# Half of the softmax scalings of an attention kernel, moved from ScalarE to GpSimd

## The chip, the cores and the metric

One core of one Trainium2 chip runs the whole program. The metric is the device time of one execution in microseconds (us); of several executions the median is given. Where a profile is read, it is one execution that the hardware profiler recorded. The engines are TensorE (PE in the rows, its weight loads PEld), VectorE (DVE), ScalarE (ACT), GpSimd (POOL), and SyncE (SP), which here issues DMAs.

## What is computed

Two layers of a gated block over 528 tokens (16 meta tokens and 512 of the input) of width 1024. Each layer normalizes, projects, and adds the output of two branches. Branch A is attention of 8 heads of 64 over one shared key and value head; a small indexer first selects for each query the 128 best visible keys. The part that the change touches is the softmax:

```python
logits = jnp.einsum('bqhd,bqkd->bqhk', qb, kg).astype(jnp.float32) * attn_scale
logits = jnp.where(valid[:, :, None, :], logits, NEG_INF)
p = jax.nn.softmax(logits, axis=-1).astype(vg.dtype)
return jnp.einsum('bqhk,bqkd->bqhd', p, vg)
```

Branch B is a pooling over several windows. Both are gated by `sigmoid(merge)` and go through an output projection. Everything is float32; the kernel splits operands of its large products into a rounded part and a residue.

## The kernel before

The dense products of a layer run one after the other on TensorE, in groups that accumulate in PSUM. Attention is not a stage of its own: it is a generator (`attention`), whose steps are pulled in between the groups of two other stages, the product of branch B (`zb`) and the gates (`mix_gates`). After each group or half group, `half_done` adds to a credit and pulls steps by it. The program order of TensorE and of VectorE is the order in which the code is traced (`tc.manual_schedule`); for ScalarE and GpSimd a scheduler puts the instructions in order by their priorities and dependences, but each instruction stays on its engine.

Attention treats four blocks of 128 queries, and in each block four pairs of heads: 16 units in a layer. Here they are numbered 0 to 15 in the first layer and 16 to 31 in the second. In block i the visible keys are n = 144, 272, 400, 528 (`NK`). For a unit (block i, pair j) the steps are:

- `logits`: TensorE, queries times keys of both heads, into PSUM banks "a".
- `soft`: VectorE adds the mask of the selection (`SC`) and takes the minimum, into the tile L of each head (128 x n in SBUF). ScalarE takes the exponential in place and sums it (line 907).
- `scale`: VectorE takes the inverse of the two sums (`rs`, line 916). ScalarE multiplies the columns from 16 on of each head's L by it, in place (line 918). The first 16 columns, the meta tokens, are multiplied into the tile `pm` (line 919), on GpSimd for the first three pairs of a block and on VectorE for the fourth.
- `turn`: TensorE transposes L in blocks of 128 columns, alternating between the two heads of the pair, into banks "a"; ScalarE copies them out (`pt`, line 934). After the fourth pair `meta_turn` does the same with `pm`.
- `values`: TensorE multiplies by the values.

One step of the generator holds the `logits` of the next unit and the `scale` of this one, the second the next unit's `soft`, the third this unit's `turn`.

In the same stretches the weights of the gates are prepared (`mixed_prep`): ScalarE rounds blocks of them (line 254), VectorE forms residues and sums of blocks, and GpSimd issues DMAs that add one block to another in SBUF (`sum_by_dma`, line 159), which are kept in program order on its queue. VectorE's instructions go through a helper that counts their cost, so all of them have line 60 in the profile, and so have TensorE's.

Of the kernel before, what the change touches and what calls it, by code (L numbers as in the profile page):

```python
# [10 lines left out]
AF = mybir.ActivationFunctionType  # L11
OP = mybir.AluOpType
# [75 lines left out]
def tile_block(ctx: ExitStack, tc: tile.TileContext, x, meta, w_in, pool_w, w_a, w_b, w_out, rows, hgain, c_tab, out):  # L88
    nc = tc.nc
    act, gp = nc.scalar, nc.gpsimd  # L90
    pe, dve = Metered(nc.tensor, pe_cost), Metered(nc.vector, dve_cost)
# [404 lines left out]
    def small(n, name):  # L496
        return tmp.tile([128, n], F32, tag=f"sm{n}", name=name, bufs=6)
# [375 lines left out]
    def attention(ensure):  # L873
        st, pvs, pms, turned = {}, {}, {}, []
# [36 lines left out]
        def scale(u):  # L911
            i, j = divmod(u, 4)
            n = NK[i]
            L, sm = st[u]
            rs = small(2, "rs")
            dve.reciprocal(rs, sm)
            for hh in range(2):
                act.activation(L[hh][:, 16:n], L[hh][:, 16:n], AF.Copy, scale=rs[:, hh:hh + 1])
                (gp if j < 3 else dve).tensor_scalar(pms[i][:, 2 * j + hh, :], L[hh][:, 0:16], rs[:, hh:hh + 1], None, op0=OP.mult)  # L919
            st[u] = L  # L920

        def turn(u):
# [43 lines left out]
        for u in range(-1, 17):  # L966
            if u + 1 < 16:
                logits(u + 1)
            if 0 <= u < 16:
                scale(u)  # L970
            yield
            if u + 1 < 16:
                soft(u + 1)
            if u >= 1:
                turned.append(u - 1)
                if u % 4 == 0 or (u > 8 and u % 2 == 0):
                    while turned:
                        values(turned.pop(0))
                if u % 4 == 0:
                    meta_values(u // 4 - 1)  # L980
            yield
            if u >= 1 and u % 4 == 0:
                gated(u // 4 - 1)
            if 0 <= u < 16:
                turn(u)
                if u % 4 == 3:
                    meta_turn(u // 4)
            yield
# [381 lines left out]
    for l in range(2):  # L1370
# [107 lines left out]
        for c in range(2):  # L1478
            w = chunk()
            for mi in range(2):  # L1480
                j = 2 * c + mi
# [42 lines left out]
        for c in (1, 0):  # L1524
            w = chunk()
            for mi in (1, 0):
                j = 2 * c + mi
# [24 lines left out]
        for c in range(2):  # L1552
            w = chunk()
            for mi in range(2):
                j = 2 * c + mi
# [26 lines left out]
        for c in range(2):  # L1582
# [3 lines left out]
            for mi in range(4):  # L1586
                j = 4 * c + mi
# [28 lines left out]
        for c in range(2):  # L1616
            w = chunk()
            for mi in range(4):
                j = 4 * c + mi
# [76 lines left out]
        else:  # L1696
            work, operands = sums_of_y(ta)
            for c in range(2):
                w = chunk()
                for t in range(1, 5):  # L1700
# [6 lines left out]
                    for e, (jj, k) in enumerate(steps):  # L1707
                        h, ww = ((hhi, w[0]), (hhi, w[1]), (hlo, w[0]))[jj]
# [60 lines left out]
```

## Time and profile before

| | us |
|---|---|
| median of 3 runs | 739.24 |
| lowest and highest | 738.99 and 739.27 |
| the profiled execution | 738.92 |
| its span, first to last instruction | 737.1 |

The granted clock of TensorE is 0.999 of full speed over the span. Busy times in the span: TensorE 727.4 us, VectorE 565.0, ScalarE 476.4, GpSimd 240.8. In the rows, a timeline's line gives the start, the duration, the engine, the line of the kernel, the operation, what it writes and reads, the sizes, how many were merged into the row, and in brackets the idle time of the engine before it with what ended that. The ends of matmuls are modelled, so matmuls overlap in the rows.

### The profile page before, as it was taken

To read this page: it belongs to the slowest core of one execution; us is meant where nothing else is said; L and a number is where in the kernel's file an instruction comes from. 1 tells how busy PE (TensorE), PEld (TensorE's weight loads), DVE (VectorE), ACT (ScalarE), POOL (GpSimd) and SP (SyncE) were. 2 spreads that over 40 slices of the span, in tenths; PEclk is the share of its full clock that TensorE was granted. 3 is DMA by queue.
4 is the path that set the end of the run, shared out by engine and by line. 5 is a ranking of instruction groups with operands and counts; after the bars stand their busy time and mean duration, and the time that the engine had idled before them with its cause. 6 is when DMAs were issued, how large, how long until landed. Compare 5 with 4: busy or idle time off the path is not lost.

```text
span 737.1 us, 15803 instructions
## 1 busy us (share of the span) xinstructions
PE 727.4 (99%) x5886; PEld 695.4 (94%) x5886; DVE 565.0 (77%) x1431; ACT 476.4 (65%) x1058; POOL 240.8 (33%) x318
## 2 busy tenths in 40 slices
PE   8999999999999999999999999999999999999998
PEld 7899999999999999999998989988989999999997
DVE  5976997889888765794549768987997777758885
ACT  5878645649878795543246687455587887864641
POOL 3850065244113120063346411751521111303500
PEclk9999999999999999999999999999999999999999
DMA  8777666777254345643604869768943544446552
GB/s 271 233 164 191 148 144 172 172 182 179 51 122 99 85 104 127 198 145 109 158 1 116 174 171 227 188 146 201 203 106 88 129 107 97 96 121 235 147 147 72
DMA packets 111036, 107.37 MB, mean 146 GB/s; under 512 B 21696, under 2 KB 93152, under 8 KB 110960
## 3 DMA queue, kind: packets, MB, share of 16 engines
q1 hardware_dynamic: 99648, 74.76, 34.2%
q0 software_dynamic: 10944, 31.46, 23.7%
q8 instruction: 46, 0.75, 0.4%
q14 instruction: 30, 0.25, 0.1%
q10 hardware_dynamic: 368, 0.15, 0.1%
HBM read 66.41 MB, written 8.49 MB: 102 GB/s over the span
## 4 chain that ended last, share of the span: by engine, by line
PE 82%; ACT 5%; DVE 4%; DMA 3%; issue 3%; POOL 2%; SPq 0%; DVEq 0%; POOLq 0%; ACTq 0%
PE d L60 66%; PE a L60 13%; PE v L60 3%; DMA raw<-s 1%; DMA raw<-in_w_in_dram 1%; ACT lt L907 1%; DVE w L60 1%; ACT w L254 1%; ACT pt L934 0%; DVE nf L60 0%; POOL t L721 0%; DVE lt L60 0%; DVE t L60 0%; POOL rk L524 0%; ACT hhi L553 0%
## 5 line engine op out<-in xcount | busy, mean ns | idle before, releaser
L60 PE MATMUL d<-hhi,w 128*128 128x256 f32 (+3 forms) x1408 | 287.5, 296 | 0.7 <-DVE rs L60 0.4
L60 PEld LDWEIGHTS d<-hhi,w 128*128 128x128 f32 x1408 | 226.0, 188 | 6.8 <-DVE c L60 0.9
L60 PE MATMUL d<-hlo,w 128*128 128x256 f32 (+3 forms) x704 | 193.6, 294 | 0.0
L60 PEld LDWEIGHTS d<-hlo,w 128*128 128x128 f32 x704 | 132.8, 189 | 2.5 <-issue 0.2
L60 DVE TENSOR_TENSOR w<-raw,w 128x512 fp32r<-128x512 f32 (+1 forms) x128 | 106.6, 853 | 5.2 <-ACT w L254 4.9
L60 PE MATMUL d<-hsum,w 128*128 128x264 f32 (+1 forms) x576 | 76.6, 286 | 0.3 <-ACT p L1143 0.3
L60 PEld LDWEIGHTS d<-hsum,w 128*128 128x128 f32 x576 | 71.7, 188 | 0.9 <-ACT p L1143 0.5
L60 PE MATMUL d<-w,hhi 128*128 128x256 f32 x496 | 72.4, 286 | 0.0
L221 POOL DMA_DIRECT2D w<-raw x42 | 37.4, 903 | 100.3 <-ACT w L220 84.1
L60 PEld LDWEIGHTS d<-w,hhi 128*128 128x128 f32 x496 | 64.1, 188 | 4.0 <-issue 1.8
L254 ACT CAST w<-raw 128x512 fp32r<-128x512 f32 x96 | 57.2, 626 | 4.1 <-DMA raw<-s 4.1
L159 POOL DMA_DIRECT2D raw<-s x17 | 15.0, 883 | 125.2 <-DVE s L60 42.1
L60 DVE MATCH_REPLACE8 sc<-m,sc 128x400 f32<-128x400 f32 (+2 forms) x100 | 54.3, 549 | 0.0
L60 DVE MAX8 m<-sc 128x8 f32<-128x400 f32 (+2 forms) x100 | 52.7, 557 | 0.8
L907 ACT ACTIVATE lt<-lt,mn,NR 128x144 f32<-128x144 f32 (+3 forms) x64 | 42.4, 666 | 15.9 <-DVE mn L60 15.9
L919 POOL TENSOR_SCALAR pm<-lt,rs 128x16 f32<-128x16 f32 x48 | 22.7, 489 | 81.8 <-DVE rs L60 74.3
L220 ACT ACTIVATE w<-raw 128x1024 fp32r<-128x1024 f32 x42 | 44.1, 1063 | 7.5 <-PE d L60 7.5
L60 PE MATMUL d<-mhi,w 128*128 128x272 f32 (+2 forms) x192 | 47.6, 328 | 0.0
L225 ACT CAST w<-raw 128x1024 fp32r<-128x1024 f32 x42 | 43.7, 1050 | 0.0
L1627 POOL TENSOR_TENSOR hlo<-ta,hhi 128x256 fp32r<-128x256 f32 (+1 forms) x28 | 28.2, 1018 | 42.1 <-PE d L60 28.9
L60 PE MATMUL d<-w,hlo 128*128 128x256 f32 x248 | 38.5, 281 | 0.0
L60 PE MATMUL d<-ahi,w 128*128 128x256 f32 (+1 forms) x256 | 36.0, 282 | 0.0
(265 smaller groups left out, 1542.0 us busy)
## 6 DMA issues: line engine op xcount, KB each, us to landing
w<-raw POOLq DMA_DIRECT2D x42, 512.0 KB, 5.9
raw<-in_w_in_dram SPq DMA_DIRECT2D x40, 512.0 KB, 4.9
raw<-in_w_in_dram SPq DMA_DIRECT2D x72, 256.0 KB, 3.3
raw<-in_w_out_dram SPq DMA_DIRECT2D x16, 512.0 KB, 3.7
raw<-in_w_branch_b_dram SPq DMA_DIRECT2D x8, 512.0 KB, 4.8
raw<-raw POOLq DMA_DIRECT2D x16, 256.0 KB, 4.2
raw<-s POOLq DMA_DIRECT2D x16, 256.0 KB, 3.3
raw<-in_w_branch_a_dram SPq DMA_DIRECT2D x8, 512.0 KB, 3.8
```

The lines of the kernel that those rows point to most:

```text
L60: return fn(*a, **k)
L159: tc.keep_in_program_order(gp.dma_start(to, x, accum_op=OP.add))
L220: act.activation(t, raws[c][s], AF.Copy, scale=-1.0)
L221: gp.dma_start(t, raws[c][s], accum_op=OP.add)
L225: act.copy(t, raws[c][s])
L254: act.copy(t[:, 0], blk[src[n]])
L907: act.activation(L[hh][:, :n], L[hh][:, :n], AF.Exp, scale=NR[:, i, h:h + 1], bias=mn[:, hh:hh + 1], accum_out=sm[:, hh:hh + 1])
L919: (gp if j < 3 else dve).tensor_scalar(pms[i][:, 2 * j + hh, :], L[hh][:, 0:16], rs[:, hh:hh + 1], None, op0=OP.mult)
L1627: pool_end = gp.tensor_sub(hlo[:, j, a:a + n], d, f(hhi[:, j, a:a + n]))
```

## The change

In `scale`, the second head's multiplication of the columns from 16 on goes to GpSimd as a tensor_scalar with the same operands. The first head's stays on ScalarE. The two narrow multiplications into `pm` stay on their engines and are traced after both wide ones, where before each stood behind the wide one of its own head.

```diff
             for hh in range(2):
-                act.activation(L[hh][:, 16:n], L[hh][:, 16:n], AF.Copy, scale=rs[:, hh:hh + 1])
-                (gp if j < 3 else dve).tensor_scalar(pms[i][:, 2 * j + hh, :], L[hh][:, 0:16], rs[:, hh:hh + 1], None, op0=OP.mult)
+                if hh:
+                    gp.tensor_scalar(L[hh][:, 16:n], L[hh][:, 16:n], rs[:, hh:hh + 1], None, op0=OP.mult)
+                else:
+                    act.activation(L[hh][:, 16:n], L[hh][:, 16:n], AF.Copy, scale=rs[:, hh:hh + 1])
+            for hh in range(2):
+                h = 2 * j + hh
+                (gp if j < 3 else dve).tensor_scalar(pms[i][:, h, :], L[hh][:, 0:16], rs[:, hh:hh + 1], None, op0=OP.mult)
             st[u] = L
```

## Rows read from the trace of the kernel before

**Rows 1.** The page's busy times, share of the span, and instructions, by engine.

```profile
PE 727.4 (99%) x5886; PEld 695.4 (94%) x5886; DVE 565.0 (77%) x1431; ACT 476.4 (65%) x1058; POOL 240.8 (33%) x318
```

**Rows 2.** Table by stretches: busy us and instructions by engine, clock, DMA share, GB/s.

```profile
170.00:290.00 120.00, 119.71 (x1058) 117.22 (x1057) 93.39 (x273) 97.70 (x247) 25.82 (x41) 1.00 0.45 103
530.00:650.00 120.00, 118.76 (x965) 111.98 (x965) 93.00 (x271) 98.32 (x240) 27.32 (x43) 1.00 0.48 107
sum 240.00, PE 238.47 PEld 229.21 DVE 186.40 ACT 196.02 POOL 53.14; mean PE 119.24 PEld 114.60 DVE 93.20 ACT 98.01 POOL 26.57
```

**Rows 3.** Timeline of TensorE in the second layer's stretch.

```profile
582.50 0.35 PE L60 MATMUL d<-hhi,w 128*128 128x256 f32 x1 [0.36 <-DVE rs L60]
...
618.36 0.51 PE L60 MATMUL a<-KK,qq 128*128 128x256 f32 x2 [0.75 <-ACT ptm L952]
618.71 1.58 PE L60 MATMUL d<-hsum,w 128*128 128x256 f32 x12
```

**Rows 4.** The same two stretches, line 918 alone: the row of sums.

```profile
sum 240.00, ACT 32.91; mean ACT 16.46
```

**Rows 5.** Line 919: duration in ns, least, median and most.

```profile
L919 POOL TENSOR_SCALAR pm<-lt,rs x48: 318/328/1192, 173.8 to 634.6; 128x16 f32<-128x16 f32 x48
```

**Rows 6.** GpSimd's groups by form: count, busy us, mean ns, idle before.

```profile
L1539 POOL TENSOR_TENSOR us<-us 128x541 f32<-128x541 f32 x6 | 6.5, 1090 | 0.5
...
L1542 POOL TENSOR_TENSOR us<-us,consts 128x16 f32<-128x16 f32 x8 | 1.8, 223 | 0.5
```

**Rows 7.** Timeline around the scaling of unit 15, several engines.

```profile
272.23 0.90 POOL L159 DMA_DIRECT2D raw<-s  x1 [5.95 <-ACT pt L934]
272.35 0.16 DVE L60 RECIPROCAL rs<-sm 128x2 f32<-128x2 f32 x1
...
272.83 1.20 POOL L159 DMA_DIRECT2D raw<-raw  x1
...
273.76 0.69 DVE L60 TENSOR_TENSOR w<-raw,w 128x512 fp32r<-128x512 f32 x1
...
274.47 1.03 PE L60 MATMUL a<-consts,lt 128*128 128x128 f32 x8
```

**Rows 8.** Waits of ScalarE in the second stretch: us, times, longest.

```profile
ACT w L254 <- DMA raw<-s: 0.7, 2, 0.4
```

**Rows 9.** Timeline of VectorE and GpSimd at two places.

```profile
169.24 1.44 DVE L60 TENSOR_SCALAR NR<-RQ 128x8 f32<-128x8 f32 x1
169.57 1.07 POOL L721 TENSOR_TENSOR t<-t,t 128x256 f32<-128x256 f32 x1
...
264.60 1.27 DVE L60 TENSOR_TENSOR w<-raw,w 128x512 fp32r<-128x512 f32 x2
264.80 1.49 POOL L919 TENSOR_SCALAR pm<-lt,rs 128x16 f32<-128x16 f32 x2 [5.29 <-DVE rs L60]
```

**Rows 10.** Timeline around the scaling of unit 23.

```profile
582.27 0.16 DVE L60 TENSOR_SCALAR NR<-RQ 128x8 f32<-128x8 f32 x1
582.34 0.16 DVE L60 RECIPROCAL rs<-sm 128x2 f32<-128x2 f32 x1
582.42 1.21 POOL L159 DMA_DIRECT2D raw<-raw  x1
...
583.75 0.42 DVE L60 SCALAR_TENSOR_TENSOR zb<-th,zb 128x256 f32<-128x256 f32 x1
...
583.97 0.60 PE L60 MATMUL a<-consts,lt 128*128 128x128 f32 x4
```

**Rows 11.** Timeline around the scaling of unit 21.

```profile
568.78 0.15 DVE L60 RECIPROCAL rs<-sm 128x2 f32<-128x2 f32 x1
...
570.28 0.69 DVE L60 TENSOR_TENSOR w<-raw,w 128x512 fp32r<-128x512 f32 x1
...
570.97 0.60 PE L60 MATMUL a<-consts,lt 128*128 128x128 f32 x4
```

**Rows 12.** Timeline around the scaling of unit 31.

```profile
643.19 0.16 DVE L60 RECIPROCAL rs<-sm 128x2 f32<-128x2 f32 x1
...
646.38 1.03 PE L60 MATMUL a<-consts,lt 128*128 128x128 f32 x8
```

## Prediction

> **What bounds the kernel now.** The first view is the page's line of busy times: TensorE is busy for 727.4 of 737.1 us [rows 1]. The second is the table by stretches for the two places where the changed lines run, one for each layer, 120 us long each. TensorE is busy for 119.71 and 118.76 us in them, ScalarE for 97.70 and 98.32, VectorE for 93.39 and 93.00, GpSimd for 25.82 and 27.32 [rows 2]. So in the stage of the change TensorE sets the time, and what it lacks to fullness is 0.29 + 1.24 = 1.53 us. Work that leaves ScalarE can give back no more than TensorE's waits. The third view, TensorE's timeline, shows the largest of these: 0.75 us before the logits of unit 29 at 618.36, released by a ScalarE copy, and 0.36 us at 582.50, released by VectorE [rows 3]. The ends of matmuls are modelled: twelve in a row take 1.58 us, so one follows the other after about 0.12 us while one alone is drawn with 0.28 [rows 3]. A wait can therefore be up to 0.16 us longer than its gap; with some five waits in the two stretches, 1.53 + 5 x 0.16 = 2.3 us is the most that there is to win.
>
> **What the change removes.** 32 of the 64 scalings on ScalarE. All 64 take 32.91 us, so about 16.5 us leave ScalarE, 8.2 in each stretch of 120 [rows 4]. One takes 32.91 / 64 = 0.51 us on average, and what follows it in ScalarE's queue (casts of weights, copies of transposed probabilities, the next exponentials) can start that much earlier, until ScalarE next waits for another engine. In the waits of [rows 3] little hangs on that: one was released by VectorE, and the other by a copy that stands behind the two exponentials of its unit, which had to wait for other things than a scaling. I take a gain between 0 and 2.3 us and 0.8 in the sum, since most of TensorE's waits end with work that no scaling precedes directly.
>
> **What it adds.** 32 scalings of 128, 256, 384 and 512 columns on GpSimd, eight of each size. The trace has no such instruction there. The same kind with 16 columns takes 318 ns at best and 328 in the median [rows 5]; with two tensors GpSimd takes 223 ns for 16 columns and 1090 for 541 [rows 6], which is 867 / 525 = 1.65 ns a column. From above, with that slope on top of the 0.32 us, 512 columns take 0.32 + 496 x 1.65 = 1.14 us, 384 0.93, 256 0.72 and 128 0.50. From below, with half the slope, since one tensor is read and not two: 0.73, 0.63, 0.52 and 0.41. I take the middle. The sum is 8 x (0.41 + 0.52 + 0.63 + 0.73) = 18 to 26 us, or 9 to 13 in a stretch in which GpSimd idles for over 92 [rows 2]. Room is not the question.
>
> **What it moves.** The two scalings of a unit ran one behind the other on ScalarE; now they run side by side. The narrow multiplications of a unit (16 columns) are issued behind the wide one, which costs nothing: their reader is one transpose for four units. In the last unit of each four, GpSimd had no such work; now it waits for the inverse sums there too, and the weight sums that it issues as DMAs may queue behind that wait, or it behind them. Each issue holds GpSimd for 0.9 to 1.2 us [rows 7]. A sum that is issued up to 1.1 us later lands later by as much; ScalarE's casts, which wait for the landings, sat idle for them for 0.7 us in all in the second stretch [rows 8], so most of that is covered.
>
> **Where the new instruction is late.** Every unit's transposes on TensorE alternate between the two heads, so the second transpose, 0.11 us behind the first (eight in a row take 1.03 us, so 1.03 / 8 = 0.13 at most) [rows 7], waits for GpSimd. In unit 15 the inverse sums start at 272.35 and the transposes at 274.47, so GpSimd has until 274.58. There it issues DMAs from 272.23 to 273.13 and from 272.83 to 274.03, and VectorE multiplies and subtracts two SBUF tensors until 274.45 [rows 7]. What a subtraction with two SBUF inputs does to GpSimd is in [rows 9]: two of them, back to back from 264.60 to 265.87, stretch a pair of 16-column multiplications that started at 264.80 to 1.49 us, past their end. So GpSimd's wide scaling starts between 273.13 (it goes between the two DMAs and ahead of VectorE) and 274.45, and ends between 273.86 and 275.59: TensorE waits between 0 and 1.0 us. Unit 23 (256 columns): sums at 582.34, VectorE with such pairs until 584.17, transposes from 583.97, due 584.08 [rows 10]. GpSimd ends between 582.42 + 0.52 (if it goes ahead of the DMA issue there), in time, and 584.17 + 0.72 = 584.89: 0 to 0.8 us. Unit 21: sums at 568.78, VectorE's train to 570.97, transposes from 570.97, due 571.08 [rows 11]; late by 0 to 570.97 + 0.72 - 571.08 = 0.6 us. Units 6 and 25 repeat that pattern with 0 to 0.3 each. The other 27 units have more cover. The last, unit 31, stands for them: sums at 643.19, transposes at 646.38 [rows 12], so 3.3 us to the second one, where a DMA issue and a scaling of 1.14 fit. Together 0 to 3.0 us of new waits on TensorE; I take the middle, 1.5.
>
> **The other direction of the same collision.** GpSimd also holds VectorE. An 8-column tensor_scalar, 0.16 us alone [rows 10], took 1.44 us from 169.24 on and ended at 170.68, while GpSimd's addition of two tensors ran from 169.57 to 170.64 [rows 9]. In the last unit of each four VectorE has two such narrow ones right behind the inverse sums, and behind them stand the weight residues and the next unit's minima. 32 instructions of 0.4 to 1.1 us can hold VectorE for 0 to 26 us in total, but it idles for 240 - 186.4 = 53.6 us in the two stretches [rows 2], and TensorE's products are ready ahead of it nearly everywhere; I put it into the slower rival, at nothing in the sum. The Trainium skill has this as a rule (SBUF — State Buffer, section "SBUF: two separate sides"): VectorE and GpSimd have a pair of ports in common, it is an exclusive lock, and whichever starts first keeps it for its whole instruction. By that rule the stretched pair of [rows 9] is what one expects, and the trace agrees. The rule speaks against the change; the slower rival is what it would do here.
>
> **The sum.** On the profiled execution's own time of 738.92 us (span 737.1 and 1.8 around it): 738.92 + 1.5 - 0.8 = 739.6. The median of the runs lies 0.32 above that execution, so 739.9 us.
>
> **Rivals.** (1) Slower: GpSimd loses to VectorE's trains each time. Its place is the five units named above, its price all of 1.0 + 0.8 + 0.6 + 0.3 + 0.3 = 3.0 us with no gain: 742.2. It decides from the point at which GpSimd's wide scaling ends later than the second transpose is due, about 1.7 to 2.3 us behind the inverse sums in the three units shown. For it: in each of these units VectorE is in a train of two-input instructions right then. Against: a wait of TensorE gives the others time, so that the next one gets shorter. (2) Faster: ScalarE was what the waits of TensorE hung on, through the order of its queue, and GpSimd comes in time. It wins up to 2.3 us: 736.9, likelier about 737.5. For it: ScalarE is the second busiest engine, and one of the two waits of [rows 3] ended with it. Against: a ceiling that near. (3) The engines' new load changes nothing for TensorE at all, because every unit has cover either way: 739.2, which is part of no change.
>
> **How the numbers follow.** What a measurement of this kernel can tell from no change is about 0.2%, 1.5 us: faster is below 737.8, slower above 740.7. The forecast has 0.45 and rival 3 has 0.20; both are no change, 0.65. Rival 1 has 0.25, since the collision is in the rows and only its size is open. Rival 2 has 0.10, since it needs nearly all of what there is to win. The range runs from 737.5 to 742.2, so that it takes in the slower rival's price and the faster one's likelier part.
>
> **What would show it.** In the profile after: ScalarE's busy time down by 16 to 17 us and GpSimd's up by 18 to 26; 32 scalings on GpSimd of 0.4 to 1.1 us undisturbed, and longer ones beside VectorE's trains; TensorE still busy for 117 to 120 us in both stretches, with its waits at transposes released by GpSimd in units 15, 21 and 23. I am wrong if GpSimd needs far more than 1.1 us for 512 columns, if waits turn up in many units, or if the order of the queues of ScalarE and GpSimd comes out otherwise and moves stages that have nothing to do with the scalings.

## The result, and the profile after

| | us |
|---|---|
| before, median of 4 runs | 739.25 |
| after, median of 4 runs (744.20 to 746.25) | 744.36 |
| ratio | 1.0076, 95% interval 1.0058 to 1.0093 |
| profiled execution after: span | 742.5 (before 737.1) |

The change makes the kernel 5.1 us slower. The forecast was no change, 739.9 us, and the time is above the range's end of 742.2.

The page's busy times after, which answer [rows 1]:

```profile
PE 729.0 (98%) x5886; PEld 696.1 (94%) x5886; DVE 568.2 (77%) x1431; ACT 463.6 (62%) x1026; POOL 279.5 (38%) x350
```

ScalarE lost 476.4 - 463.6 = 12.8 us, GpSimd gained 279.5 - 240.8 = 38.7. VectorE, whose instructions are the same, is busy 3.2 us longer. The two stretches of [rows 2], with the same columns:

```profile
170.00:290.00 120.00, 118.71 (x1046) 115.95 (x1045) 93.54 (x269) 89.97 (x227) 43.32 (x58) 1.00 0.45 101
530.00:650.00 120.00, 116.27 (x932) 108.68 (x932) 92.47 (x270) 89.08 (x217) 48.19 (x59) 1.00 0.48 105
```

TensorE lacks 1.29 + 3.73 us to fullness, where it lacked 0.29 + 1.24. At an unchanged clock (1.00) it waits. The new instruction, GpSimd's groups by form (count, busy us, mean ns, idle before):

```profile
L919 POOL TENSOR_SCALAR lt<-lt,rs 128x512 f32<-128x512 f32 x8 | 16.8, 2094 | 18.9 <-DVE rs L60 11.3 <-issue 6.9 <-PE a L60 0.7
...
L919 POOL TENSOR_SCALAR lt<-lt,rs 128x128 f32<-128x128 f32 x8 | 5.4, 673 | 20.2 <-DVE rs L60 20.2
```

41.4 us in all four sizes, means of 0.67 to 2.09 us, where 18 to 26 us and 0.41 to 1.14 were forecast. Yet TensorE waits for GpSimd itself in one place only, in unit 15 (timeline, several engines; compare [rows 7]):

```profile
273.67 0.16 DVE L60 RECIPROCAL rs<-sm 128x2 f32<-128x2 f32 x1
...
274.19 1.88 POOL L919 TENSOR_SCALAR lt<-lt,rs 128x512 f32<-128x512 f32 x1
...
274.48 1.26 DVE L60 TENSOR_TENSOR w<-s,w 128x512 fp32r<-128x512 f32 x1
...
276.12 0.75 PEld L60 LDWEIGHTS a<-consts,lt 128*128 128x128 f32 x7 [0.30 <-POOL lt L919]
```

The large waits are elsewhere, and other engines end them (TensorE's timeline, at the places of [rows 3] in the second layer):

```profile
618.79 0.98 PE L60 MATMUL a<-consts,lt 128*128 128x128 f32 x6 [1.18 <-DVE mn L60]
...
623.34 0.51 PE L60 MATMUL a<-KK,qq 128*128 128x256 f32 x2 [1.15 <-ACT ptm L957]
```

Before, the first did not exist and the second was 0.75 us. What stands ahead of the second one's copy on ScalarE, after and then before (timelines of ScalarE):

```profile
618.30 0.62 ACT L254 CAST w<-raw 128x512 fp32r<-128x512 f32 x1 [1.12 <-DMA raw<-s]
618.83 0.37 ACT L1148 COPY p<-d 128x256 f32<-128x256 f32 x1
619.09 1.66 ACT L254 CAST w<-raw 128x512 fp32r<-128x512 f32 x3
620.65 0.86 ACT L939 COPY pt<-a 128x512 f32<-128x512 f32 x2
...
623.03 0.26 ACT L957 COPY ptm<-a 128x128 f32<-128x128 f32 x1
```

```profile
613.35 0.37 ACT L1143 COPY p<-d 128x256 f32<-128x256 f32 x1
614.11 1.66 ACT L254 CAST w<-raw 128x512 fp32r<-128x512 f32 x3 [0.40 <-DMA raw<-s]
615.68 0.85 ACT L934 COPY pt<-a 128x512 f32<-128x512 f32 x2
...
618.05 0.25 ACT L952 COPY ptm<-a 128x128 f32<-128x128 f32 x1
```

The diff does not touch these lines, but their order is another one. Four casts stand ahead of the copies of `pt` where there were three, and the cast that waits for the DMA now has the copy of `p` behind it. Line by line, ScalarE's order after is that of before without the second scalings, except for 27 casts of weight blocks that stand 1 to 6 places earlier, 74 places in all, ten of them in the first layer and 17 in the second (besides them, one other cast and one copy moved by two places and one). The order of TensorE, VectorE and SyncE is the same, and GpSimd's too, apart from the new instruction. The waits of ScalarE in the second stretch (us, times, longest) answer [rows 8], where this was 0.7:

```profile
ACT w L254 <- DMA raw<-s: 3.3, 4, 1.1
```

So two theories stood against each other: A, the loss is ScalarE's new order; B, it is the instruction on GpSimd. In the experiments an order was fixed by dependences on ScalarE alone, which add no wait between engines.

### The profile page after: what moved, and what is told of

The parts are those of the page before. It is cut to its first block, busy times and chain, and to the rows that moved or that the text cites. A ratio compares the mean times of both kernels' runs of the same rounds, so it can differ in the third digit from the quotient of the medians.

```text
span 742.5 us, 15820 instructions
## 1 busy us (share of the span) xinstructions
PE 729.0 (98%) x5886; PEld 696.1 (94%) x5886; DVE 568.2 (77%) x1431; ACT 463.6 (62%) x1026; POOL 279.5 (38%) x350
## 4 chain that ended last, share of the span: by engine, by line
PE 81%; ACT 7%; DVE 5%; DMA 3%; issue 3%; POOL 1%; SPq 0%; DVEq 0%; ACTq 0%; POOLq 0%
PE d L60 66%; PE a L60 12%; ACT lt L907 2%; PE v L60 2%; DMA raw<-s 2%; ACT w L254 2%; DVE w L60 1%; DVE lt L60 1%; DMA raw<-in_w_in_dram 1%; ACT pt L939 1%; DVE s L60 0%; DVE zb L60 0%; ACT c L1135 0%; DVE raw L60 0%; ACT hhi L553 0%
## 5 line engine op out<-in xcount | busy, mean ns | idle before, releaser
L919 POOL TENSOR_SCALAR lt<-lt,rs 128x128 f32<-128x128 f32 (+3 forms) x32 | 41.4, 1293 | 73.6 <-DVE rs L60 54.8
L1632 POOL TENSOR_TENSOR hlo<-ta,hhi 128x256 fp32r<-128x256 f32 (+1 forms) x28 | 28.3, 1022 | 42.5 <-PE d L60 29.8
L721 POOL TENSOR_TENSOR t<-t,t 128x256 f32<-128x256 f32 (+1 forms) x30 | 26.1, 870 | 27.5 <-DVE t L60 25.8
```

What stands on the lines that cost most here:

```text
L721: gp.tensor_tensor(t1[:m, :256], t1[:m, :256], t2[:m, :256], op=OP.add)
L919: gp.tensor_scalar(L[hh][:, 16:n], L[hh][:, 16:n], rs[:, hh:hh + 1], None, op0=OP.mult)
L1632: pool_end = gp.tensor_sub(hlo[:, j, a:a + n], d, f(hhi[:, j, a:a + n]))
```

## Experiments

Ratios are against the kernel before on the same chip; its median there was 739.16 to 739.38.

| kernel | us | ratio, 95% interval |
|---|---|---|
| relief_only | 742.78 | 1.0040, 1.0025 to 1.0054 |
| relief_old_order | 739.19 | 0.9998, 0.9988 to 1.0008 |
| changed_old_order | 740.85 | 1.0017, 1.0006 to 1.0027 |
| vector_old_order | 741.16 | 1.0023, 1.0015 to 1.0032 |
| before_new_order | 744.85 | 1.0072, 1.0058 to 1.0086 |
| before_dead_load | 740.45 | 1.0012, 1.0003 to 1.0021 |
| part_old_order | 740.53 | 1.0014, 1.0005 to 1.0023 |
| before_later_casts | 742.57 | 1.0042, 1.0029 to 1.0054 |
| two_casts_early | 740.17 | 1.0009, 1.0001 to 1.0018 |
| second_layer_order | 743.23 | 1.0048, 1.0036 to 1.0060 |
| copies_first | 738.33 | 0.9984, 0.9976 to 0.9993 |
| change_but_two | 740.46 | 1.0013, 1.0005 to 1.0022 |

### One half of the change at a time

**relief_only** takes the scaling from ScalarE and gives it to no one:

```diff
-            for hh in range(2):
-                if hh:
-                    gp.tensor_scalar(L[hh][:, 16:n], L[hh][:, 16:n], rs[:, hh:hh + 1], None, op0=OP.mult)
-                else:
-                    act.activation(L[hh][:, 16:n], L[hh][:, 16:n], AF.Copy, scale=rs[:, hh:hh + 1])
+            for hh in range(1):
+                act.activation(L[hh][:, 16:n], L[hh][:, 16:n], AF.Copy, scale=rs[:, hh:hh + 1])
```

> The changed kernel without the 32 wide scalings on GpSimd: the second head's columns from 16 on stay unscaled (that part of the computation is left out). ScalarE's instructions stand in the same order as in the changed kernel, whose order differs from the one before: casts of weight blocks (line 254) stand 1 to 11 places earlier. Theory A (the order of ScalarE's queue is what costs: a cast that waits for a DMA holds up what stands behind it): near the changed kernel, 742 to 744.5 us. Theory B (GpSimd's instruction costs: it holds VectorE, or is late itself): at or below the kernel before, 737.5 to 739.5 us.

It has less work than the kernel before and is 3.6 us slower. ScalarE's order in it is the changed kernel's to the last instruction: it is the missing scaling that reorders, not the instruction on GpSimd. (The expectation counts 1 to 11 places; instruction by instruction, without the second scalings, it is the 1 to 6 given above.) **relief_old_order** and **changed_old_order** have ScalarE's order fixed as it was before (the list `ACT_ORDER`, a number for each instruction, is left out here):

```diff
+    acts = [i for i in nc.cur_bb.bb.instructions if i.engine == mybir.EngineType.Activation]
+    order = [p + int(d) for p, d in enumerate(ACT_ORDER.split())]
+    assert len(acts) == len(order), (len(acts), len(order))
+    for p in range(1, len(order)):
+        tc.add_manual_dep(acts[order[p]], acts[order[p - 1]].name,
+                          mybir.DependencyInfo(mybir.DependencyClass.NoSync, mybir.DependencyReason.DATA),
+                          reason="ScalarE's order of the kernel before")
```

> No wide scaling of the second head anywhere (left out), ScalarE in the order of the kernel before: what ScalarE's freed 16.5 us are worth by themselves. Theories A and B both: at or below the kernel before, 737 to 739.2 us; the difference to the kernel before is the most that the change could ever give back.

> The changed kernel, with ScalarE's instructions held in the order of the kernel before (the 32 scalings that left it aside). All 32 wide scalings run on GpSimd. Theory A: the loss goes, 738.5 to 740 us. Theory B: the loss stays, 743 to 744.5 us. Both at work: between, near 741.5.

In the old order the relief is worth nothing (739.19), and the whole change costs 1.7 us in place of 5.1: between A and B, so both are at work, and A more. **before_new_order** is the converse: the kernel before, with both scalings on ScalarE, in the changed kernel's order.

> All the work of the kernel before, both scalings of a unit on ScalarE, one behind the other, and GpSimd does none of them; only ScalarE's order is that which the changed kernel has: 27 casts of weight blocks stand 1 to 6 places earlier. Theory A (the order of ScalarE's queue is most of the loss, whoever scales): the order was worth 3.6 us in the four runs so far, so 742.3 to 743.5 us, ratio about 1.005. Rival B (the early casts hurt only because the changed kernel leaves ScalarE with holes at other places; with the second scalings back between them the casts have landed when their turn comes): 739.0 to 740.5.

It takes 744.85 us, as much as the changed kernel, with no change of the work, and more than A's 743.5. So the order alone is enough for the whole loss, and the change's own parts nearly cancel in it: the order +5.5 (739.3 to 744.85), the relief -2.1 in that order (to 742.78), the instruction on GpSimd +1.6 (to 744.36), each term uncertain by about 1 us. These are three steps on one path from the kernel before to the changed one, so that they add up to the loss is no test. On the other path, with the change made in the old order first, the change costs 1.7 us and the order then 3.5. Rival B of that run (with the second scalings back, the early casts find their data) falls. The two orders and three kinds of work together:

| second head's wide scaling | old order | new order |
|---|---|---|
| on ScalarE | 739.3 | 744.85 |
| left out | 739.19 | 742.78 |
| on GpSimd | 740.85 | 744.36 |

### What an early cast does

**two_casts_early** moves only two casts, those of the ScalarE rows above:

> All the work of the kernel before, in its order of ScalarE but for two casts of weight blocks, near 613 us, which stand where the changed kernel has them: one a place earlier, ahead of the copy of p, the other six places earlier, ahead of the copies of transposed probabilities, the exponentials of unit 28 and the copy of ptm. Theory A (a cast that is brought forward costs at its own place what it takes, some 0.5 us, and what it has to wait for its DMA, to the copies and exponentials behind it): 739.8 to 740.6 us, and TensorE's wait at the logits of unit 29, 0.75 us in the kernel before, longer by 0.5 to 1.0. Rival B (no single cast matters; the loss builds up because the casts of a whole layer run ahead of the weights' DMAs): 739.0 to 739.5, and that wait as before.

ScalarE and, as the last line, TensorE in its timeline:

```profile
614.47 0.62 ACT L254 CAST w<-raw 128x512 fp32r<-128x512 f32 x1 [0.67 <-DMA raw<-s]
615.00 0.36 ACT L1143 COPY p<-d 128x256 f32<-128x256 f32 x1
615.26 1.66 ACT L254 CAST w<-raw 128x512 fp32r<-128x512 f32 x3
...
619.51 0.50 PE L60 MATMUL a<-KK,qq 128*128 128x256 f32 x2 [1.26 <-ACT ptm L952]
```

The logits of unit 29 wait 1.26 us, 0.51 more than in [rows 3]. That is one more cast ahead of the copy that empties their bank, 0.53 us from start to start (614.47 to 615.00). The time follows: +0.7 us by the ratio, 0.1 to 1.3 by its interval. Theory A holds at this place; the rival, that no single cast matters, falls. **second_layer_order**, the new order from the second layer on, costs 3.9 us of the 5.5:

> All the work of the kernel before; ScalarE's order of before in the first layer and of the changed kernel in the second, where 17 of the 27 casts stand early. TensorE's waits with the changed order in both layers grew by 1.0 us at one place of the first layer and by 2.9 at five of the second. Theory A (each place costs by itself): 743 to 744 us, some 4 to 4.5 of the 5.5. Rival B (the layers are not independent: what is lost in the first is part of the second's loss): under 742.

743.23 lies in A's bounds, though 3.9 us is just under A's 4 to 4.5, and it leaves about 1.6 us to the first layer's ten casts if the places add up.

How the places may add up: ScalarE, VectorE and the sums by DMA form a ring in the second layer, in which each waits for the one before. One round of the chain of waits in the changed kernel (start, us, what; most pieces left out):

```profile
584.58 3.36 DMA raw<-s
...
589.12 0.88 ACT w L254 x2
...
590.16 1.53 ACT lt L907 x4
...
593.24 1.20 DVE w L60 x2
...
595.72 1.52 ACT lt L907 x4
...
599.74 3.28 DMA raw<-s
```

From one DMA sum the chain goes through casts, exponentials, VectorE's weight work and minima, and the next exponentials to the next DMA sum, and TensorE is no part of it from 570 to 623 us. Before, it is in the chain from 582.5 to 594.6 without a gap. GpSimd's issues of these sums give a round's length, after and then before:

```profile
569.89 0.89 POOL L159 DMA_DIRECT2D raw<-s  x1 [7.09 <-DVE s L60]
...
584.58 0.90 POOL L159 DMA_DIRECT2D raw<-s  x1 [6.25 <-DVE s L60]
...
599.74 0.89 POOL L159 DMA_DIRECT2D raw<-s  x1 [4.89 <-DVE s L60]
...
614.93 0.89 POOL L159 DMA_DIRECT2D raw<-s  x1 [5.79 <-DVE s L60]
```

```profile
568.10 0.90 POOL L159 DMA_DIRECT2D raw<-s  x1 [8.71 <-DVE s L60]
...
581.83 0.90 POOL L159 DMA_DIRECT2D raw<-s  x1 [7.06 <-DMA raw<-in_w_in_dram]
...
595.88 0.90 POOL L159 DMA_DIRECT2D raw<-s  x1 [7.00 <-ACT pt L934]
...
610.69 0.90 POOL L159 DMA_DIRECT2D raw<-s  x1 [7.81 <-ACT pt L934]
```

Three rounds take 45.0 us after and 42.6 before. The length goes with the order more than with the work: by the same rows it is 45.1 us in before_new_order and 44.6 in relief_only, but 42.5 in relief_old_order and 43.4 in changed_old_order. In each of the three rounds one early cast stands ahead of the exponentials (at 574.53, 589.64 and 604.09 us) and another ahead of the activation of `c` behind them (line 1135). TensorE falls behind with the ring: the logits of unit 29 come 5.0 us later than before (618.36 to 623.34). That this is how the single waits become the sum is read from the chain; no run opened the ring by itself.

Is a cast best put off, then? **before_later_casts** moves 20 of the 27 the other way, by 48 places:

> All the work of the kernel before, with 20 of the 27 casts that the change brought forward moved back instead, by 1 to 6 places each, 48 places in all: the same size as the change's, in the other direction. Theory A (a cast that stands in ScalarE's queue ahead of its data holds what is behind it, and that alone is the cost of the order): not slower than before, and up to 0.7 us faster, the time for which ScalarE still sat at such casts: 738.4 to 739.3. Rival B (the order is tuned on both sides: any cast that is moved costs, since weights that come late stop TensorE's products too): 740 to 743.

It loses 3.3 us: the second half of that run's A, that only early casts cost, falls. TensorE's wait for the copy of `ptm` stays (0.74 us), and beside it TensorE now waits most at the products, 0.75 us for VectorE at 583.67 and again at 647.30, and 0.77 for a ScalarE copy at 664.53. So both orders that were tried around the old one are slower. It is not the best all the same. **copies_first** takes from [rows 3] what TensorE waits for and moves that copy, and one copy of `pt` at 247 us:

> All the work of the kernel before, and two copies moved forward in ScalarE's order where TensorE's logits wait for the bank that they empty: the copy of ptm ahead of the two exponentials of unit 28 (TensorE waits 0.75 us for it at 618.36), and a copy of transposed probabilities ahead of the copy of u (0.20 us at 247.84). If ScalarE's order is what these waits hang on, they go, and the time falls by up to 0.9 us: 738.3 to 739.0. Rival: the exponentials are then 0.16 us later and another wait takes over: 739.0 to 739.6.

ScalarE and, as the last line, TensorE in its timeline:

```profile
616.68 0.28 ACT L952 COPY ptm<-a 128x128 f32<-128x128 f32 x1
616.84 0.84 ACT L907 ACTIVATE lt<-lt,mn,NR 128x528 f32<-128x528 f32 x1
...
616.98 1.14 PE L60 MATMUL a<-KK,qq 128*128 128x272 f32 x8
```

The wait of 0.75 us is gone (all eight logits in a row). At 738.33 us, ratio 0.9984, it beats both kernels, with not one instruction more or less. The wait at 247 us did not go; it is 0.4 us there.

### What the instruction on GpSimd costs

**before_dead_load** adds to the kernel before an instruction on GpSimd whose result no one reads:

```diff
+            gi = gp.tensor_scalar(consts[:, 328:312 + n], consts[:, 328:312 + n], ones, None, op0=OP.mult)
```

> All the work of the kernel before, in its order of ScalarE, and beside it, right behind the inverse sums of each unit, a multiplication of 128 to 512 columns by 1.0 on GpSimd, in place, on a table that no one waits for: the load of the change without its result. Theory A (what the instruction on GpSimd costs is not that it ends late but that VectorE and GpSimd's other work are held while it runs): 740.3 to 741.3 us, the 1.7 us of the changed kernel in the old order, and the same VectorE instructions prolonged by some 3 us in sum. Rival B (it costs because TensorE waits for its result): 739.0 to 739.5, and TensorE's waits as in the kernel before.

It costs 1.1 us (0.2 to 1.6 by its interval) where the changed kernel in the old order costs 1.7 (0.4 to 2.0), so by the medians most of the price is not lateness. In unit 11 (GpSimd, VectorE, and TensorE's next logits in their timelines):

```profile
242.75 1.26 POOL L917 TENSOR_SCALAR consts<-consts,ones 128x384 f32<-128x384 f32 x1 [2.65 <-DVE rs L60]
...
242.89 1.00 DVE L60 TENSOR_TENSOR w<-raw,w 128x512 fp32r<-128x512 f32 x1
...
248.70 0.50 PE L60 MATMUL a<-KK,qq 128*128 128x256 f32 x2 [0.71 <-ACT pt L938]
```

VectorE's weight residue takes 1.00 us beside GpSimd. Without it, in the kernel before, with TensorE's next logits:

```profile
242.34 0.69 DVE L60 TENSOR_TENSOR w<-raw,w 128x512 fp32r<-128x512 f32 x1
...
247.84 1.34 PE L60 MATMUL a<-KK,qq 128*128 128x256 f32 x6 [0.20 <-ACT pt L934]
```

The minima, exponentials and copies behind it come later, and TensorE waits 0.71 us where it waited 0.20. Ten VectorE instructions are so prolonged, by 3.0 us in sum against the kernel before; in the changed kernel it is the same ten, also by 3.0 us. The load holds GpSimd's own queue too: the second DMA sum of a pair is issued 1.74 us behind the first (583.07 to 584.81), where it was 0.59 (581.83 to 582.42). From 170 to 680 us no compute engine is shown waiting for a second sum. ScalarE's waits for first ones grow from 4.1 to 4.4 us, and SyncE, whose loads wait for second ones, does so for 15.5 us in place of 14.0. No run separates this from VectorE's part. **vector_old_order** lets VectorE do the scaling itself:

> The second head's wide scaling on VectorE instead of GpSimd, ScalarE in the order of the kernel before. Theory A: 738 to 739.5 us. Theory B (the instruction's length on the path through VectorE counts, 32 of about 0.25 to 0.45 us): 739.5 to 741.5 us, less than with GpSimd, since VectorE is held for a shorter time.

In unit 11 that takes VectorE 0.42 us, about what GpSimd's instruction makes it lose, and TensorE's wait is 0.76. The time is 741.16, in B's bounds, but not less than with GpSimd, as B had it. **part_old_order** gives GpSimd only 128 columns:

> The change for 128 columns only: of the second head's columns GpSimd scales the first 128 (about 0.6 us by the changed kernel's row), ScalarE the rest, in the old order of ScalarE. GpSimd's load is then 32 x 0.6 = 19 us in place of 41. Theory A (the price goes by the time for which GpSimd holds or delays the others): about half of 1.7 us, 739.8 to 740.3. Rival B (each wait for GpSimd costs, whatever its length): 740.6 to 741.2. Rival C (only the long ones, of 384 and 512 columns, cost): 739.0 to 739.5.

GpSimd is busy 23 us more in place of 38, VectorE's prolongation falls to 0.9 us, and yet the time is 740.53: between A and B, and no run separates them, since the intervals of this group overlap. C's 739.0 to 739.5 is missed. **change_but_two** takes out the units 11 and 27, where TensorE's wait had been longest:

```diff
-                if hh:
+                if hh and u != 11:
```

> The change with ScalarE's order of before, but in units 11 and 27 the second head's wide scaling stays on ScalarE too. In these two units the instruction on GpSimd runs beside VectorE's work on weights just ahead of the next minima (1.00 and 1.09 us in place of 0.67), and TensorE then waits 0.5 and 0.65 us longer in the dead load and in the changed kernel in the old order alike. Theory A (the price of the instruction on GpSimd is VectorE being held in these two units): 739.2 to 739.9 us. Rival B (it is the sum of many small delays over 32 units): 740.5 to 741.

740.46 is above A's range and just under B's. Against changed_old_order these two units give back 0.3 us by the ratios and 0.6 by the medians, with each ratio uncertain by 0.7 us. So the price of 1.1 to 1.7 us does not seem to sit in the two units that I could point to; where it sits stays open.

## Why the prediction was wrong

- **The step that failed** is one that had no term. "What follows it in ScalarE's queue can start that much earlier" took ScalarE's order as fixed. The description of the kernel says that a scheduler makes it; the prediction names this only as its last way to be wrong, with no price. Measured: +5.5 us with the work of before, +3.5 with that of the change. What one cast costs could have been read from rows of before: it holds ScalarE for 0.52 us, and where TensorE waits for a ScalarE copy already [rows 3], nothing covers a cast that comes in front of that copy. How many casts would move could not be read there.
- **The relief** was put at 0.8 (0 to 2.3). It is 0 in the old order and 2.1 in the one that the kernel got. The ceiling of 2.3 from TensorE's waits was not passed; that the relief would win anything only once the order had made new waits was not seen.
- **GpSimd** was put at +1.5 by lateness in five units. Measured +1.6 (1.7 in the old order), but by another way, so the agreement is luck. Lateness appeared in unit 15 alone, 0.30 us. The load without its result, which holds VectorE (the collision's other direction, "at nothing in the sum") and GpSimd's own queue, has 1.1 us. VectorE's idle time of 53.6 us did not cover it: in unit 11 the prolonged instruction stands ahead of the next minima and exponentials.
- **GpSimd's duration**: the bounds of 0.73 to 1.14 us for 512 columns were too low; the shortest is 1.57 us, the mean 2.09. The upper slope, 1.65 ns a column from an instruction with two tensors [rows 6], was no bound: with one tensor and a pointer for the scalar the least times of the four sizes (0.60, 0.92, 1.24, 1.57) rise by 2.5 ns a column. The durations were not what failed, though: TensorE waited for the result once.
- **A reading of [rows 9]** was short. VectorE's narrow instruction at 169.24 began 0.33 us before the addition that was said to hold it. Another GpSimd instruction was running then, until 169.94:

```profile
168.56 1.38 POOL L524 TENSOR_TENSOR RQ<-RQ,mhalf 128x4 f32<-128x4 f32 x1
```

- **Rival 1** had the right sign at a chance of 0.25, by a mechanism that gives little of it. The range had no room for the reorder.

## What to carry to other kernels

Where a scheduler makes one engine's order, removing an instruction from it is an edit of everything on that engine: compare the order of the two builds, fix the old order, and only then price the edit. In a kernel whose busiest engine is 99% full, ask of each instruction of 0.5 us on another engine which bank, copy or DMA stands behind it; moving two copies gained 1.0 us, where moving 13 us of work off the same engine lost 5.1. An engine with idle time is not free if what its instruction disturbs stands in a chain that the busiest one waits for.

## What the hardware showed

GpSimd's tensor_scalar of 512 float32 columns took 1.57 us at the least; VectorE, in vector_old_order, did the same eight in 0.50 on average. The Trainium skill (GPSIMD Engine Reference, section 3.1) gives a best case of 769 ns for 512 elements on GpSimd, and section 4.1 calls one-input work there roughly line-rate. Here it is twice the first, and three times VectorE's; the measurement decides.

While GpSimd and VectorE overlap, VectorE is longer, and in unit 15 GpSimd too (1.88 us, 1.57 being the least; in unit 11 of the dead load 1.26, 1.23 being the least of its 384 columns). In unit 15 VectorE's instruction began 0.29 us after GpSimd's and ended at 275.74, before GpSimd's at 276.07. In unit 11 of the dead load it ended at 243.89, GpSimd's at 244.01. The rule of the Trainium skill in the prediction (SBUF — State Buffer, section "SBUF: two separate sides"), that the loser of the shared ports blocks for the other's whole instruction, would have had VectorE start its work at GpSimd's end. By the 0.68 and 0.69 us that the two took before, they would have ended at 276.75 and 244.70, 1.0 and 0.8 us later than they did. These rows show them longer by 0.58 and 0.31 us and no such block, as far as spans on GpSimd, which are rough, can tell.
